# Output projection of a decoder layer: seven half-size products per pair of row blocks instead of eight

## The chip, the core and the metric

The kernel runs on one core of a Trainium2 chip. A core has five engines, each with a queue of its own that is worked off in order: TensorE (PE in the profile; PEld is its loading of weights), VectorE (DVE), ScalarE (ACT), GpSimd (POOL) and SyncE (SP), which here issues all DMA transfers. An engine that meets an instruction whose operands are not ready waits, and so does everything that is queued behind it. Engines wait for each other by semaphores. Matmuls write to PSUM, eight banks of 128 x 512 float32; everything else lies in SBUF.

The metric is the device time of one execution in microseconds (us).

## What is computed

One decoder layer on a sequence of 4096 rows of width 1024. Cut to what matters here:

```python
q_a, k_a, v_a, g_a, q_b, k_b, v_b, g_b, r_b = split_cols(x @ w_in, IN_SPLITS)
out_a = sliding_window_attention(rope(q_a), rope(k_a), v_a, sinks) * silu(g_a)   # 512 columns
out_b = norm(gla_chunked(q_b, k_b, v_b, log_a)) * silu(g_b)                      # 512 columns
mix = concatenate([out_a, out_b]) @ w_out                                        # (4096 x 1024) @ (1024 x 1024)
x = layer_norm(ALPHA * x + mix, ln_g, ln_b)
```

All of it is float32. A matmul takes its operands as float32r, a shorter form, so the kernel splits each operand into a rounded part h and the rest l and adds three products, hh + hl + lh.

## The kernel before

The 4096 rows are 32 blocks of 128 (NB = 32). Three stages follow each other: sliding-window attention over all blocks, gated linear attention (GLA) over all blocks, and then the output projection with residual and layer norm, which is what the change rewrites.

The first two stages leave their halves of the projection's input, transposed, in DRAM: `mixd[n][0]` and `mixd[n][1]`, each 128 x 4 x 128, for block n. The projection then takes one block after another (lines 729 to 764). It loads both halves into `mr` and the block's residual rows into `xr`; `split` makes `mh` (a cast on ACT, line 98) and `ml` (a subtraction on DVE, line 103). For each half of the 1024 output columns `project` (line 128) runs 8 chunks of 3 matmuls of 128 x 512 into one PSUM bank, `py`: 48 matmuls a block. DVE adds ALPHA times the residual from the bank (line 745) and takes statistics (746, 747); `rsqrt_eps` (767) is a few one-column instructions on DVE and ACT. Then ACT scales the block (761), POOL multiplies by `lg` (762), DVE adds `lb` (763), and SP stores it (764). The last block does its tail on DVE in two halves (755, 756).

The weights of the projection are loaded by `load_group` (line 106) near the end of the GLA stage, one half of the columns after `b_split_v` of the last block and one after its `b_gate`: 16 raw tiles, each with a cast on ACT and a subtraction on DVE or POOL.

Tiles come from pools with a fixed number of buffers for each tag. A tile whose buffer is still in use waits for its last reader: `xraw`, `xh` and `xl` have two buffers each, `xr` and `y` two, each PSUM tag (`pj`, `tp`, `c`, `d`) two. Code is written in program order, and a scheduler then sets the order of each engine's queue; the queue is fixed when the program is built.

Of the kernel before, what the change touches and what calls it, by code (L numbers as in the profile page):

```python
# [9 lines left out]
F32 = mybir.dt.float32  # L10
F32R = mybir.dt.float32r
# [8 lines left out]
P = 128  # L20
D = 1024
# [16 lines left out]
# column groups of the input projection, in the order the host lays them out  # L38
# [3 lines left out]
# constant columns: identity, cumulative-sum matrix, halves, causal mask, attention masks  # L42
# [8 lines left out]
def layer_kernel(  # L51
# [23 lines left out]
    xp = ctx.enter_context(tc.tile_pool(name="xp", bufs=2))  # L75
    ps = ctx.enter_context(tc.tile_pool(name="ps", bufs=2, space=PSUM))
# [18 lines left out]
    def split(hdst, ldst, src, heng, leng):  # L95
        """src = hdst + ldst exactly: a rounded part and the rest."""
# [8 lines left out]
    # ---- weights: slot s of chunk k holds (h, l) of one column group  # L105
    def load_group(wr, src, c0, n, slot, width, early=False):
        hs, ls = [], []
        for k in range(NK):
            raw = wr.tile([P, 512], F32, tag="wraw", name=f"wraw{slot}_{k}")
# [18 lines left out]
    def project(dst, x, wg, n, k0=0, k1=NK):  # L128
        """Chunks k0..k1 of one column group's product with a block of rows."""
        hs, ls = wg  # L130
        for k in range(k0, k1):
            a, b = x[0][:, k, :], x[1][:, k, :]
            pe.matmul(dst[:, :n], a, hs[k][:, :n], start=(k == 0), stop=False)  # L133
            pe.matmul(dst[:, :n], a, ls[k][:, :n], start=False, stop=False)  # L134
            pe.matmul(dst[:, :n], b, hs[k][:, :n], start=False, stop=(k == NK - 1))  # L135

    # ================= sliding-window attention =================
    with ExitStack() as pa:
        wr = pa.enter_context(tc.tile_pool(name="wra", bufs=6))
# [9 lines left out]
        wkv = load_group(wr, w_a, 512, 256, 1, 272, True)  # L149

        # rotary tables: [position in block, block, (cos | cos)], (sin | sin)
# [31 lines left out]
        # ---- constants  # L183
# [14 lines left out]
        # ---- up-projection of the decay, bias as one more row; rows: (h, b_h), h, (l, b_l), l  # L198
# [31 lines left out]
        def a_kv(n, pkv, qk):  # L230
            """Rotary; the values' parts."""
# [19 lines left out]
        def a_turn_k(n, kk):  # L251
            """Keys with dims on the partitions, twice."""
# [8 lines left out]
        def a_turn_q(n, qk):  # L261
            """Queries with dims on the partitions, (h ; l) stacked."""
# [21 lines left out]
        def a_scores(n, qs):  # L284
            """Four steps, one for each bank of two heads; the last gives the probabilities."""
# [109 lines left out]
        for n in range(NB):  # L395
# [19 lines left out]
            if n == NB - 2:  # L415
                wb["q"] = load_group(wr, w_b, 0, 272, 1, 272)
# [430 lines left out]
```

## Time and profile before

| | us |
|---|---|
| median of three runs | 1766.86 |
| lowest and highest | 1766.32, 1768.08 |
| span of the profiled execution | 1766.5 |
| PE busy in it | 1733.4 (98%) |
| DVE busy | 1057.4 (60%) |
| ACT busy | 802.2 (45%) |
| POOL busy | 457.0 (26%) |

The profiled execution ran within 0.4 us of the median, so sums are made against its span. Shares of the whole span are averages over three stages: attention to about 670 us, GLA to about 1405 us, the projection from there on. The granted clock of PE is full in nearly all slices. Since matmuls are pipelined, the duration of a matmul's row is longer than the time that one costs; the distance between starts shows that.

### The profile page before, as it was taken

How to read it: one execution, taken by the hardware profiler on the slowest of the kernel's cores; microseconds unless marked ns; L12 is line 12 of the kernel's file. 1: busy time of each engine (PE TensorE's matmuls, PEld its weight loads, DVE VectorE, ACT ScalarE, POOL GpSimd, SP SyncE). 2: the span in 40 equal slices, each digit the busy share in tenths (PEclk: the TensorE clock that was granted, in tenths of full speed). 3: DMA queues.
4: the chain of work that ended last, by engine and by line, in shares of the span. 5: the costliest groups of instructions: out<-in, count | busy, mean ns of one | idle time of the engine just before them, and what ended most of it. 6: DMA issues, size and time to landing. Idle time of an engine off the chain costs nothing.

```text
span 1766.5 us, 27174 instructions
## 1 busy us (share of the span) xinstructions
PE 1733.4 (98%) x9978; PEld 1503.2 (85%) x9978; DVE 1057.4 (60%) x2738; ACT 802.2 (45%) x2032; POOL 457.0 (26%) x633
## 2 busy tenths in 40 slices
PE   7999999999999999999999999999999899999998
PEld 5788888888888887899999999999999788888886
DVE  6766666666666677555555555555555655555555
ACT  5555554555555466444444444444444622222221
POOL 3222222222222243322222222222222412222221
PEclk9999999999999999999999999999999999999999
DMA  6211111111111132111111111111111354444442
GB/s 202 90 37 37 37 37 42 48 37 37 37 37 37 43 103 69 34 37 37 37 37 37 37 37 37 37 37 37 37 37 37 114 171 145 146 147 148 144 143 83
DMA packets 48649, 120.00 MB, mean 68 GB/s; under 512 B 5698, under 2 KB 9092, under 8 KB 48516
## 3 DMA queue, kind: packets, MB, share of 16 engines
q1 hardware_dynamic: 48516, 118.27, 20.2%
q8 instruction: 78, 1.28, 0.3%
q14 instruction: 55, 0.45, 0.1%
HBM read 84.70 MB, written 33.55 MB: 67 GB/s over the span
## 4 chain that ended last, share of the span: by engine, by line
PE 57%; DVE 1%; DMA 0%; ACT 0%; issue 0%; POOL 0%; DVEq 0%; ACTq 0%
PE py L133 7%; PE py L135 7%; PE py L134 7%; PE bv L133 3%; PE bg L133 3%; PE bg L135 3%; PE bg L134 3%; PE bv L134 3%; PE bv L135 3%; PE bq L133 2%; PE bq L134 2%; PE bq L135 2%; PE bk L135 2%; PE bk L134 2%; PE bk L133 2%; PE to L669 1%
## 5 line engine op out<-in xcount | busy, mean ns | idle before, releaser
L134 PE MATMUL py<-wl,mh 128*128 128x512 f32 x512 | 199.9, 390 | 0.0
L135 PE MATMUL py<-wh,ml 128*128 128x512 f32 x512 | 199.8, 390 | 0.0
L133 PE MATMUL py<-wh,mh 128*128 128x512 f32 x512 | 199.8, 390 | 0.0
L339 POOL TENSOR_SCALAR s<-s,rec 128x256 f32<-128x256 f32 x256 | 124.4, 502 | 280.4 <-DVE ngm L327 217.4
L331 ACT ACTIVATE s<-s,ngm 128x256 f32<-128x256 f32 x256 | 127.2, 498 | 137.6 <-DVE ngm L327 132.7
L762 POOL TENSOR_TENSOR y<-y,lg 128x1024 f32<-128x1024 f32 x31 | 74.3, 2396 | 268.1 <-ACT y L761 253.4
L100 POOL TENSOR_SCALAR xh<-xraw 128x512 fp32r<-128x512 f32 x126 | 78.6, 641 | 203.6 <-PE pg L134 191.7
L520 POOL TENSOR_TENSOR qp<-bqs,ee 128x256 f32<-128x256 f32 x32 | 24.3, 759 | 377.2 <-ACT ee L515 365.1
L314 DVE CUSTOM_DVE_ANT_0 s<-psc,msk 128x256 f32<-128x256 f32 x256 | 97.9, 420 | 31.2 <-PE psc L304 30.3
L103 DVE TENSOR_TENSOR pl<-pt,ph 128x512 fp32r<-128x512 f32 x128 | 85.6, 688 | 49.6 <-ACT ph L98 47.4
L135 PEld LDWEIGHTS py<-wh,ml 128*128 128x128 f32 x512 | 96.5, 188 | 20.1
L134 PEld LDWEIGHTS py<-wl,mh 128*128 128x128 f32 x512 | 96.4, 188 | 20.0
L133 PEld LDWEIGHTS py<-wh,mh 128*128 128x128 f32 x512 | 96.5, 189 | 19.8
L133 PE MATMUL pg<-wh,xh 128*128 128x512 f32 x256 | 112.5, 440 | 0.8 <-DVE vv L247 0.8
L133 PE MATMUL pq<-wh,xh 128*128 128x512 f32 x256 | 104.5, 408 | 6.3 <-ACT wh L98 6.1
L98 ACT CAST ph<-pt 128x512 fp32r<-128x512 f32 x128 | 72.1, 588 | 84.5 <-PE pt L353 82.8
L135 PE MATMUL pq<-wh,xl 128*128 128x512 f32 x256 | 103.3, 403 | 3.3 <-DVE xl L103 3.3
L133 PE MATMUL bg<-wh,xh 128*128 128x512 f32 x256 | 106.1, 414 | 0.0
L133 PE MATMUL bv<-wh,xh 128*128 128x512 f32 x256 | 105.4, 412 | 0.0
L98 ACT CAST mh<-mr 128x1024 fp32r<-128x1024 f32 x32 | 33.7, 1054 | 155.3 <-PE py L134 155.3
L134 PE MATMUL pq<-wl,xh 128*128 128x512 f32 x256 | 103.0, 402 | 0.1
L135 PE MATMUL pg<-wh,xl 128*128 128x512 f32 x256 | 101.1, 395 | 0.0
(224 smaller groups left out, 5126.5 us busy)
## 6 DMA issues: line engine op xcount, KB each, us to landing
xraw<-in_xt_dram SPq DMA_DIRECT2D x64, 512.0 KB, 3.5
mr<-mx SPq DMA_DIRECT2D x64, 256.0 KB, 3.5
xr<-in_xn_dram SPq DMA_DIRECT2D x32, 512.0 KB, 3.5
out_dram<-y SPq DMA_DIRECT2D x31, 512.0 KB, 2.6
mx<-att SPq DMA_DIRECT2D x32, 256.0 KB, 2.0
mx<-mb SPq DMA_DIRECT2D x32, 256.0 KB, 2.1
wraw<-in_w_a_dram SPq DMA_DIRECT2D x16, 256.0 KB, 4.4
wraw<-in_w_b_dram SPq DMA_DIRECT2D x16, 256.0 KB, 3.9
```

Of the source, the lines that this page charges most:

```text
L98: act.copy(hdst, src)
L100: pool.tensor_scalar(hdst, src, 1.0, 1.0, ALU.mult, ALU.mult)
L103: leng.tensor_tensor(ldst, src, hdst, ALU.subtract)
L133: pe.matmul(dst[:, :n], a, hs[k][:, :n], start=(k == 0), stop=False)
L134: pe.matmul(dst[:, :n], a, ls[k][:, :n], start=False, stop=False)
L135: pe.matmul(dst[:, :n], b, hs[k][:, :n], start=False, stop=(k == NK - 1))
L314: dve.tensor_tensor_reduce(out=s, in0=psc[:, e * 256 : (e + 1) * 256], in1=mask, scale=0.125, scalar=NEG, op0=ALU.add, op1=ALU.max, accum_ ...
L331: act.activation(sc[i], sc[i], AF.Exp, bias=ngm[:, h : h + 1], accum_out=den[:, h : h + 1])
L339: pool.tensor_scalar(sc[i], sc[i], rec[:, h : h + 1], 1.0, ALU.mult, ALU.mult)
L520: pool.tensor_tensor(qp, B[n]["q"], ee, ALU.mult)
L669: pe.transpose(to[:, hs], og[:, hs], ident)
L762: pool.tensor_tensor(y, y, lg, ALU.mult)
```

## The change

Two row blocks are now taken together. The pair's input is a 2 x 2 arrangement A of pieces with 128 rows and 512 columns (a11, a12 of the even block, a21, a22 of the odd one), the weights a 2 x 2 arrangement B of 512 x 512. One level of Strassen's scheme, in Winograd's form, gives the four output pieces from seven products instead of eight. It needs four sums of pieces of A in each pair (s1 to s4), four of pieces of B (once, when the weights are loaded), and seven on the output side, of which three are made by letting a second product accumulate in the bank of a first one.

- **Weights.** `w_split` makes seven operands (h, l) for each of four chunks: 28 casts on ACT, 28 subtractions on DVE and 16 sums on POOL, instead of 16 casts and 16 subtractions. Chunks 0 and 1 come in the last GLA block, chunk 2 after it, chunk 3 when the projection's pools are open.
- **A pair's input.** `pair_load` loads both blocks and makes the sums on POOL; `pair_parts` makes seven (h, l) pieces of 128 x 512 in two buffers of `xh` and `xl`; `pair_late` makes the last three of them later.
- **Products.** `product` is 4 chunks of 3 matmuls: 84 matmuls for a pair.
- **Output.** `residual` loads the two blocks' rows into `y` itself and scales them by ALPHA on ACT. u1 is a copy of the first bank (ACT), u2 and u3 are running sums (DVE); three sums onto `y` are made on POOL, four on DVE. The layer norm is as before.
- **Elsewhere.** The GLA weights for q and k become one group of 528 columns, loaded at the seam of the first two stages (k's was loaded in block 2 before). Some buffers change their number: `wra` 6 to 5, `wrb` 3 to 4, `ah`, `al`, `gw` 2 to 1, `y` 2 to 4.

```diff
-    wkv = load_group(wr, w_a, 512, 256, 1, 272, True)
+    wkv = load_group(wr, w_a, 512, 256, 1, 528, True)
...
-                wb["q"] = load_group(wr, w_b, 0, 272, 1, 272)
-            if n == 2:
-                wb["k"] = load_group(wr, w_b, 272, 256, 3, 256)
+                wb["qk"] = load_group(wr, w_b, 0, 528, 1, 528)
...
+        def w_split(k, q, extra=None):
+            r11, r12, r21, r22 = q
...
+            part(0, r11, dve)
+            pool.tensor_tensor(r11, r12, r11, ALU.subtract)
+            pool.tensor_tensor(r12, r22, r12, ALU.subtract)
+            part(6, r22, dve)
+            pool.tensor_tensor(r22, r22, r11, ALU.subtract)
+            part(3, r11, dve)
+            part(4, r21, dve)
+            pool.tensor_tensor(r21, r21, r22, ALU.subtract)
+            part(2, r12, dve)
+            part(1, r22, dve)
+            part(5, r21, dve)
...
+        def pair_parts(p, i, srcs):
+            h = xp.tile([P, NK, P], F32R, tag="xh", name=f"mh{p}_{i}")
+            l = xp.tile([P, NK, P], F32R, tag="xl", name=f"ml{p}_{i}")
+            for c, src in zip((lo, hi), srcs):
+                split(h[:, c], l[:, c], src, act, dve)
+            return [(h[:, c], l[:, c]) for c, _ in zip((lo, hi), srcs)]
+
+        def pair_load(p):
+            ra = xp.tile([P, NK, P], F32, tag="xraw", name=f"ma{p}")
+            rb = xp.tile([P, NK, P], F32, tag="xraw", name=f"mb{p}")
+            for r, n in ((ra, 2 * p), (rb, 2 * p + 1)):
+                sp.dma_start(r[:, :4, :], mixd[n][0])
+                sp.dma_start(r[:, 4:, :], mixd[n][1])
...
+            pool.tensor_tensor(s1, rb[:, lo], rb[:, hi], ALU.add)
+            pool.tensor_tensor(s2, s1, ra[:, lo], ALU.subtract)
+            pool.tensor_tensor(rb[:, lo], ra[:, lo], rb[:, lo], ALU.subtract)
+            parts = pair_parts(p, 0, (ra[:, lo], s2))
+            pool.tensor_tensor(s2, ra[:, hi], s2, ALU.subtract)
+            parts += pair_parts(p, 1, (rb[:, lo], s1))
+            return parts, (ra[:, hi], rb[:, hi], s2)
+
+        def pair_late(p, made):
+            parts, (a12, a22, s4) = made
+            return parts + pair_parts(p, 2, (a12, a22)) + pair_parts(p, 3, (s4,))
...
             if last:
-                wo[0] = load_group(wr, w_o, 0, 512, 0, 512)
+                w_split(0, w_load(wr, 0))
             pk = bank("pj", f"bk{n}")
-            project(pk, x, wb["k"], 256)
+            project(pk, x, wb["qk"], 256, off=272)
+            if last:
+                w_split(1, w_load(wr, 1))
...
+        first = pair_load(0)
+        w_split(2, w_load(wr, 2))
         b_out(NB - 1)
         b_store(NB - 1)
...
+        w_split(3, w_load(wr, 3), c1)
...
+                y = c4.tile([P, D], F32, tag="y", name=f"y{n}")
+                sp.dma_start(y, xn[n * P : (n + 1) * P, :])
+                act.mul(y, y, ALPHA)
...
+                b7, b5 = bank("c", f"b7_{p}"), bank("d", f"b5_{p}")
+                b2, b3, b4 = b1, b5, b7
+                product(b1, made[0][0], 0)
+                product(b6, made[0][1], 1)
+                ops = pair_late(p, made)
+                product(b7, ops[2], 2)
+                product(b5, ops[3], 3)
+
+            act.copy(u1, b1)
+            dve.tensor_tensor(u2, u1, b6, ALU.add)
+            dve.tensor_tensor(u3, u2, b7, ALU.add)
+
+            pool.tensor_tensor(y1[:, HI], y1[:, HI], u3, ALU.add)
+            dve.tensor_tensor(y1[:, HI], y1[:, HI], b5, ALU.add)
+            stats(n1, y1, st1, 1)
+            pool.tensor_tensor(y1[:, LO], y1[:, LO], u2, ALU.add)
+            pool.tensor_tensor(y0[:, HI], y0[:, HI], u2, ALU.add)
+            if p + 1 < NB // 2:
+                nxt = pair_load(p + 1)
...
+                product(b2, ops[4], 4, more=True)
+                product(b4, ops[5], 5, more=True)
+                product(b3, ops[6], 6, more=True)
+            dve.tensor_tensor(y0[:, LO], y0[:, LO], b2, ALU.add)
+            stats(n0, y0, st0, 0)
+            dve.tensor_tensor(y1[:, LO], y1[:, LO], b4, ALU.add)
+            stats(n1, y1, st1, 0)
+            normed(n1, y1, st1)
+            dve.tensor_tensor(y0[:, HI], y0[:, HI], b3, ALU.add)
+            stats(n0, y0, st0, 1)
+            normed(n0, y0, st0, p == NB // 2 - 1)
```

What stands in the queues, once with blocks 23 to 25 before and pairs 11 to 13 after (blocks 22 to 26); lines are those of each kernel's own file. First SP's queue in the middle of the projection, before: `mr` are a block's two input halves, `xr` its residual rows.

```order
L731 DMA mr24_18379<-mx24_0_117 128x512
L732 DMA mr24_18379<-mx24_1_118 128x512
L764 DMA out_0_dram<-y20_18064 128x1024
L734 DMA xr23_18301<-in_xn_dram 128x1024
L731 DMA mr25_18460<-mx25_0_119 128x512
L732 DMA mr25_18460<-mx25_1_120 128x512
L764 DMA out_0_dram<-y21_18145 128x1024
```

SP's queue in the middle of the projection after the change: `ma` and `mb` are the inputs of a pair's even and odd block, `y26` and `y27` receive residual rows.

```order
L853 DMA out_0_dram<-y23_18462 128x1024
L733 DMA ma13_18719<-mx26_0_124 128x512
L853 DMA out_0_dram<-y22_18459 128x1024
L734 DMA ma13_18719<-mx26_1_125 128x512
L733 DMA mb13_18720<-mx27_0_126 128x512
L734 DMA mb13_18720<-mx27_1_127 128x512
L827 DMA y26_18817<-in_xn_dram 128x1024
L827 DMA y27_18820<-in_xn_dram 128x1024
```

Before, a store of block 20 or 21 stands among loads for blocks 23 to 25. Now three of pair 13's four input loads stand right behind the store of block 22, which is written while pair 12 is worked on.

POOL's queue at the change from the GLA stage to the projection, before (from `y0` on there is one such row for each block, and nothing else):

```order
L103 TENSOR_TENSOR wl2_3_16327<-wraw2_3_16324,wh2_3_16326 128x512
L103 TENSOR_TENSOR wl2_5_16339<-wraw2_5_16336,wh2_5_16338 128x512
L626 TENSOR_TENSOR gw31_16298<-gw31_16298,gs31_16297 128x512
L103 TENSOR_TENSOR wl2_7_16351<-wraw2_7_16348,wh2_7_16350 128x512
L762 TENSOR_TENSOR y0_16444<-y0_16444,lg_16431 128x1024
L762 TENSOR_TENSOR y1_16525<-y1_16525,lg_16431 128x1024
```

POOL's queue in one pair of the projection after the change (the same nine rows come again for each pair from the third on):

```order
L737 TENSOR_TENSOR s1_12_18546<-mb12_18541 128x512
L738 TENSOR_TENSOR s2_12_18547<-s1_12_18546,ma12_18540 128x512
L739 TENSOR_TENSOR mb12_18541<-ma12_18540,mb12_18541 128x512
L741 TENSOR_TENSOR s2_12_18547<-ma12_18540,s2_12_18547 128x512
L851 TENSOR_TENSOR y23_18462<-y23_18462,lg_16480 128x1024
L891 TENSOR_TENSOR y25_18641<-y25_18641,u2_12_18647 128x512
L892 TENSOR_TENSOR y24_18638<-y24_18638,u2_12_18647 128x512
L851 TENSOR_TENSOR y22_18459<-y22_18459,lg_16480 128x1024
L888 TENSOR_TENSOR y25_18641<-y25_18641,u3_12_18648 128x512
```

Two multiplications by `lg` in a pair have become nine instructions, and those of pair 11's blocks (22 and 23) now stand behind the input sums of pair 12 and around its first output sums.

DVE's queue around the addition of `lb` (line 763) in the middle of the projection, before:

```order
L760 SCALAR_TENSOR_TENSOR nb22_18292<-mv22_18228,crs22_18284 128x1
L745 SCALAR_TENSOR_TENSOR y23_18307<-xr23_18301,py23_0_18310 128x512
L763 TENSOR_TENSOR y22_18226<-y22_18226,lb_16432 128x1024
L746 BN_STATS cst23_18308<-y23_18307 128x6
L745 SCALAR_TENSOR_TENSOR y23_18307<-xr23_18301,py23_1_18337 128x512
L746 BN_STATS cst23_18308<-y23_18307 128x6
L103 TENSOR_TENSOR ml25_18466<-mr25_18460,mh25_18465 128x1024
```

DVE's queue around the two additions of `lb` (now line 852) for blocks 23 and 22, after the change; `cnt`, `crs` and `nb` are one-column steps of the norm, the `ml12` the l parts of pair 12's last pieces:

```order
L921 TENSOR_TENSOR cnt22_18625<-crs22_18624 128x1
L922 SCALAR_TENSOR_TENSOR cnt22_18625<-cnt22_18625,mv22_18622 128x1
L923 SCALAR_TENSOR_TENSOR crs22_18624<-cnt22_18625,crs22_18624 128x1
L849 SCALAR_TENSOR_TENSOR nb22_18632<-mv22_18622,crs22_18624 128x1
L885 TENSOR_TENSOR u2_12_18647<-u1_12_18646,b6_12_18650 128x512
L852 TENSOR_TENSOR y23_18462<-y23_18462,lb_16481 128x1024
L104 TENSOR_TENSOR ml12_2_18678<-ma12_18540,mh12_2_18677 128x512
L104 TENSOR_TENSOR ml12_2_18678<-mb12_18541,mh12_2_18677 128x512
L852 TENSOR_TENSOR y22_18459<-y22_18459,lb_16481 128x1024
L886 TENSOR_TENSOR u3_12_18648<-u2_12_18647,b7_12_18651 128x512
L889 TENSOR_TENSOR y25_18641<-y25_18641,b5_12_18652 128x512
```

The end of the previous pair's layer norm (blocks 22 and 23) now stands between u2 and u3 of pair 12, and ahead of the l parts that the pair's last three products read.

## Rows read from the trace of the kernel before

**Rows 1.** The page, part 1: busy us (share, instructions) by engine.

```profile
PE 1733.4 (98%) x9978; PEld 1503.2 (85%) x9978; DVE 1057.4 (60%) x2738; ACT 802.2 (45%) x2032; POOL 457.0 (26%) x633
```

**Rows 2.** The chain of waits from 1390 us to the end, shares by line.

```profile
by line: PE py L133 30.7%; PE py L135 30.7%; PE py L134 30.6%; DMA wraw<-in_w_o_dram 1.0%; issue 0.6%; DVE wl L103 0.6%; DVE og L659 0.4%; DVE nt L772 0.4%; DVE y L755 0.4%; ACT wh L98 0.3%; DVE y L756 0.2%; DVE cst L746 0.2%; DVE btl L103 
```

**Rows 3.** Twenty blocks: us; PE, PEld, DVE, ACT, POOL busy (x); clock, DMA, GB/s.

```profile
1443.80:1661.40 217.60, 217.60 (x962) 180.18 (x961) 118.69 (x241) 54.06 (x81) 47.93 (x20) 1.00 0.43 145
```

**Rows 4.** Waits of that stage: engine, line, releaser; us, times, longest.

```profile
POOL y L762 <- ACT y L761: 229.1, 27, 8.5
...
DVE y L745 <- PE py L135: 69.1, 55, 1.4
```

**Rows 5.** Timeline of PE, projection: start us, duration us, instruction.

```profile
1561.13 0.39 PE L133 MATMUL py<-wh,mh 128*128 128x512 f32 x1
...
1561.81 0.39 PE L133 MATMUL py<-wh,mh 128*128 128x512 f32 x1
```

**Rows 6.** Groups by form, those twenty blocks: busy us, mean ns, idle before.

```profile
L762 POOL TENSOR_TENSOR y<-y,lg 128x1024 f32<-128x1024 f32 x20 | 47.9, 2396 | 169.7 <-ACT y L761 169.7
L746 DVE BATCH_NORM_STATS2 cst<-y 128x6 f32<-128x512 f32 x41 | 28.3, 691 | 0.7
...
L761 ACT ACTIVATE y<-y,nb,crs 128x1024 f32<-128x1024 f32 x20 | 24.9, 1243 | 16.2 <-DVE nb L760 16.2
L763 DVE TENSOR_TENSOR y<-y,lb 128x1024 f32<-128x1024 f32 x20 | 24.5, 1226 | 35.0 <-POOL y L762 35.0
...
L772 DVE TENSOR_TENSOR cnt<-crs 128x1 f32<-128x1 f32 x20 | 3.2, 160 | 10.1 <-ACT crs L771 10.1
```

**Rows 7.** Groups by form, loading of projection weights, 1370 to 1412 us.

```profile
L103 POOL TENSOR_TENSOR wl<-wraw,wh 128x512 fp32r<-128x512 f32 x8 | 10.7, 1335 | 11.2 <-ACT wh L98 11.2
L98 ACT CAST wh<-wraw 128x512 fp32r<-128x512 f32 x16 | 9.8, 617 | 7.1 <-DMA wraw<-in_w_o_dram 6.7 <-PE bv L135 0.4
L103 DVE TENSOR_TENSOR wl<-wraw,wh 128x512 fp32r<-128x512 f32 x8 | 7.6, 951 | 3.6 <-ACT wh L98 3.5
```

**Rows 8.** The tile `wl` there: ns min/median/max, first and last start.

```profile
L103 DVE TENSOR_TENSOR wl<-wraw,wh x8: 670/693/1705, 1381.5 to 1408.5; 128x512 fp32r<-128x512 f32 x8
L103 POOL TENSOR_TENSOR wl<-wraw,wh x8: 1282/1292/1634, 1383.0 to 1410.8; 128x512 fp32r<-128x512 f32 x8
```

**Rows 9.** Timeline of DVE in that stretch.

```profile
1393.68 2.37 DVE L103 TENSOR_TENSOR wl<-wraw,wh 128x512 fp32r<-128x512 f32 x2
...
1408.46 0.67 DVE L103 TENSOR_TENSOR wl<-wraw,wh 128x512 fp32r<-128x512 f32 x1
1409.06 0.67 DVE L103 TENSOR_TENSOR al<-am,ah 128x512 fp32r<-128x512 f32 x1
```

**Rows 10.** Timeline of POOL in that stretch.

```profile
1393.87 1.63 POOL L103 TENSOR_TENSOR wl<-wraw,wh 128x512 fp32r<-128x512 f32 x1 [3.02 <-ACT wh L98]
...
1408.67 2.21 POOL L626 TENSOR_TENSOR gw<-gw,gs 128x512 f32<-128x512 f32 x1 [0.87 <-ACT gs L619]
```

**Rows 11.** The tile `st` in the GLA stage: ns min/median/max.

```profile
L535 DVE TENSOR_SCALAR st<-tot,dd x62: 272/514/760, 729.3 to 1397.6; 128x128 f32<-128x128 f32 x62
```

**Rows 12.** DMA issues of the projection: KB each, median us to landing.

```profile
out_dram<-y SPq DMA_DIRECT2D x28, 512.0 KB, 2.6
...
mr<-mx SPq DMA_DIRECT2D x52, 256.0 KB, 3.6
```

**Rows 13.** Timeline of SP's queue, one issue in the projection.

```profile
1565.63 0.42 SPq L732 DMA_DIRECT2D mr<-mx  x1
```

**Rows 14.** Columns as in Rows 3, just behind a wait of PE.

```profile
1405.00:1408.40 3.40, 3.40 (x12) 2.90 (x11) 3.40 (x6) 3.40 (x7) 1.29 (x1) 0.50 0.60 216
```

**Rows 15.** Waits of PE, 1380 to 1420 us.

```profile
PE pat L576 <- ACT qbh L561: 3.6, 1, 3.6
```

**Rows 16.** Timeline of the kernel's end.

```profile
1758.10 0.39 PE L135 MATMUL py<-wh,ml 128*128 128x512 f32 x1
...
1762.85 0.99 SPq L757 DMA_DIRECT2D out_dram<-y  x2
```

More of the change, by code (lines that the diff above doesn't have):

```diff
@@ L126, in load_x, with project @@
         return h, l
[L128 removed]
+    def project(dst, x, wg, n, k0=0, k1=NK, off=0):
         hs, ls = wg
+        c = slice(off, off + n)
         for k in range(k0, k1):
             a, b = x[0][:, k, :], x[1][:, k, :]
[L133 to L135 removed]
+            pe.matmul(dst[:, :n], a, hs[k][:, c], start=(k == 0), stop=False)
+            pe.matmul(dst[:, :n], a, ls[k][:, c], start=False, stop=False)
+            pe.matmul(dst[:, :n], b, hs[k][:, c], start=False, stop=(k == NK - 1))
     with ExitStack() as pa:
[L139 removed]
+        wr = pa.enter_context(tc.tile_pool(name="wra", bufs=5))
         e1 = pa.enter_context(tc.tile_pool(name="e1", bufs=1))
@@ L728, in layer_kernel, with product, residual, stats @@
         sp.dma_start(lb, ln_b.partition_broadcast(P))
-        for n in range(NB):
-            raw = xp.tile([P, NK, P], F32, tag="xraw", name=f"mr{n}")
-            sp.dma_start(raw[:, :4, :], mixd[n][0])
-            sp.dma_start(raw[:, 4:, :], mixd[n][1])
-            xr = c2.tile([P, D], F32, tag="xr", name=f"xr{n}")
-            sp.dma_start(xr, xn[n * P : (n + 1) * P, :])
-            mh = xp.tile([P, NK, P], F32R, tag="xh", name=f"mh{n}")
-            ml = xp.tile([P, NK, P], F32R, tag="xl", name=f"ml{n}")
-            split(mh, ml, raw, act, dve)
-            y = c2.tile([P, D], F32, tag="y", name=f"y{n}")
-            st = c2.tile([P, 2, 6], F32, tag="st", name=f"cst{n}")
-            mv = c2.tile([P, 2], F32, tag="mv", name=f"mv{n}")
-            for i in range(2):
-                s = slice(512 * i, 512 * i + 512)
-                py = bank(("pj", "tp")[n % 2], f"py{n}_{i}")
-                project(py, (mh, ml), wo[i], 512)
-                dve.scalar_tensor_tensor(y[:, s], xr[:, s], ALPHA, py, ALU.mult, ALU.add)
-                dve.bn_stats(st[:, i, :], y[:, s])
+        def product(dst, x, op, k0=0, k1=4, more=False):
+            xh_, xl_ = x
+            for k in range(k0, k1):
+                h, l = wo[k][op]
+                a, b = xh_[:, k, :], xl_[:, k, :]
+                pe.matmul(dst, a, h, start=(not more and k == 0), stop=False, skip_group_check=more)
+                pe.matmul(dst, a, l, start=False, stop=False, skip_group_check=more)
+                pe.matmul(dst, b, h, start=False, stop=(k == 3), skip_group_check=more)
+        LO, HI = slice(0, 512), slice(512, 1024)
+        def residual(p):
+            ys = []
+            for i in range(2):
+                n = 2 * p + i
+                y = c4.tile([P, D], F32, tag="y", name=f"y{n}")
+                sp.dma_start(y, xn[n * P : (n + 1) * P, :])
+                act.mul(y, y, ALPHA)
+                ys.append(y)
+            return ys
+        def stats(n, y, st, i):
+            dve.bn_stats(st[:, i, :], y[:, 512 * i : 512 * i + 512])
+        def normed(n, y, st, tail=False):
+            mv = c2.tile([P, 2], F32, tag="mv", name=f"mv{n}")
             dve.bn_aggr(mv, st.rearrange("p a b -> p (a b)"))
@@ L751, in layer_kernel @@
             rows = slice(n * P, (n + 1) * P)
-            if n == NB - 1:
-                for i in range(2):
-                    s = slice(512 * i, 512 * i + 512)
+            if tail:
+                for s in (LO, HI):
                     dve.scalar_tensor_tensor(y[:, s], y[:, s], mv[:, 0:1], lg[:, s], ALU.subtract, ALU.mult)
```

75 lines of the change are left out of this document (64 added, 11 removed).

## The prediction

> **What bounds the kernel now.** First the page's busy shares: PE works 98% of the span [rows 1]. Then the chain of waits from 1390 us on: three matmul lines of `project` carry 92% of it, so in the projection nothing but PE sets the time [rows 2]. Then twenty blocks in its middle: 217.60 us, or 10.88 us a block, PE busy in all of them, at full clock (2.4 GHz), while DVE is busy for 118.7 us, ACT for 54.1 and POOL for 47.9 [rows 3]. The waits there are of engines that wait for PE, or for each other behind it [rows 4]. Starts of matmuls three apart lie 0.68 us apart, so one costs 0.2267 us, whatever its row says [rows 5]; 96 in two blocks make 21.76, which is the 2 x 10.88 above. The other engines have half their time free, but the change takes from PE and gives to them, so I need what two blocks ask of each, and in which order.
>
> **What it removes.** 12 of 96 matmuls per pair of blocks: 84 x 0.2267 = 19.04 us instead of 21.76. If PE stayed the bound that is 16 x 2.72 = 43.5 us.
>
> **What it adds, as busy time.** Per pair POOL gets seven sums of 128x512 (four input, three output) beside its two multiplications by `lg`. Such an instruction takes 1.29 us undisturbed [rows 8], `lg` 2.40 [rows 6]: 7 x 1.29 + 2 x 2.40 = 13.8 us. That is under 19, and DVE's and ACT's sums are too. By shares alone the change would pay.
>
> **What the shares don't show: DVE and POOL hold each other up.** Subtractions of one kind in one stretch take between 0.67 and 1.7 us on DVE, and 1.28 to 1.63 on POOL [rows 8]. The timelines tell which: two on DVE took 2.37 us together when a POOL instruction started 0.2 us after the first one [rows 9, 10]; and where two ran on DVE back to back at 0.67 each, from 1408.46 on, POOL's `gw`, started 0.2 us behind the first, took 2.21 us, that is 1.29 and the rest of both [rows 9, 10]. A small `tensor_scalar` of GLA shows the same: 0.27 us at best, 0.51 median, 0.76 at most [rows 11]. So I count a DVE instruction with two SBUF inputs and a two-input POOL instruction as excluding each other, the later one waiting for the whole of the earlier and for what DVE runs directly behind. DVE instructions that read PSUM or one input stay at 0.69 in all of the projection [rows 6], and I leave them free.
>
> The Trainium skill ("SBUF — State Buffer", section "Who interferes with whom") says that a DVE instruction with two SBUF inputs contends with a GpSimd instruction that reads SBUF, and that the loser "fully blocks" rather than slowing down. The single rows agree; the group's mean, 951 ns beside a median of 693 [rows 7, 8], reads like a partial price of 0.26 us. By the rule a pair takes about 29 us, by the mean about 24.3.
>
> Of that exclusive time a pair needs, beside POOL's 13.8, seven subtractions of 0.69, two additions of `lb` at 1.23 and eight one-column steps at 0.16 [rows 6, 8]: 8.6 on DVE, together 22.4 us. That alone is over PE's 19.04, and over the 21.76 of before, where the same sum is 4.8 + 6.2 = 11.0.
>
> **The chain through a pair.** It isn't only a sum: the queues tie it into a loop. From the order of the queues in a pair, with durations of rows:
> (a) DVE adds `lb` to the even block of the pair before, 1.23 [rows 6].
> (b) SP waits for that to store the block; behind the store stand three of the next pair's four input loads. Issues are 0.4 apart [rows 13], and a load lands 3.6 after its issue, a store of 512 KB taking 2.6 beside it [rows 12]: 3 x 0.4 + 3.6 = 4.8 at least; all four transfers share the same engines, so I take 5.6 (bounds 4.6 and 6).
> (c) POOL makes s1 and s2, both of which need the last load: 2 x 1.29, and half a microsecond behind DVE: 3.1.
> (d) ACT casts s2: 0.62 [rows 7].
> (e) DVE: half a microsecond behind POOL's third sum, then three subtractions, three statistics at 0.69, an addition from the bank at 0.69 and seven small steps, up to `nb` of the odd block; less what back-to-back instructions overlap (0.6 instead of 0.69 from start to start [rows 9]): 5.7.
> (f) ACT scales the odd block: 1.24 [rows 6].
> (g) POOL multiplies it by `lg`: 2.40. Meanwhile DVE's small steps for the even block stand still.
> (h) DVE: those small steps, u2, `lb` of the odd block, two subtractions, one behind the other: 0.8 + 0.69 + 1.23 + 1.3, less overlap 3.7. POOL's sums with u2 stand still behind them.
> (i) POOL: two sums with u2, then `lg` of the even block: 2 x 1.29 + 2.40 = 5.0. Then (a) again.
> Sum: 1.23 + 5.6 + 3.1 + 0.62 + 5.7 + 1.24 + 2.40 + 3.7 + 5.0 = 28.6, and nine handovers of about 0.05: **29 us a pair**. Bounds: 27.3 with the loads at 4.6 and no half microsecond in (c) or (e) where the other engine happens to be done, 29.9 with loads at 6 and one more sum delayed. The first pairs are lighter, since no norm stands before them; on average I take 28.7. Against 21.76 that is 6.9 us more in each of some 14 intervals: **+97 us** (bounds +78 and +114). PE's busy time falls by 43.5 us as planned, and this buys nothing: PE waits some 9.7 us in each pair.
>
> **From GLA into the projection.** Before, 16 subtractions were shared by DVE and POOL there. Now 28 on DVE (0.69) and 16 sums on POOL (1.29) exclude each other: 19.3 + 20.6 = 40 us where before it was 16. They stand in the last blocks of GLA, whose own chain has DVE and POOL steps, and before the first products, which need all chunks; chunk 3's loads stand behind the store of block 31's GLA part. I take **+22** (bounds +8, if most of the 24 us runs beside GLA's matmuls, and +30).
>
> **The end.** Before, 8.4 us passed from the start of the last matmul to the end of the span [rows 16]. The last product is now followed by the odd block's norm ahead of the even one's on DVE, about 5 us of statistics, small steps and half-size sums; and before that the last pair's products wait as in any pair. **+11** (bounds +3, +14).
>
> **Elsewhere.** k's GLA weights are loaded with q's at the seam rather than in block 2; nothing waited long at either place: **-3** (bounds -6, +3). Casts on ACT and the ALPHA multiplications (0.62 and 1.24 at most) lie beside DVE's work in (e); if that is shorter they come onto the path, one microsecond a pair at most.
>
> Sum: 1766.5 + 97 + 22 + 11 - 3 = 1893.5, and with the 0.4 us that the median lies above the profiled span about **1895**.
>
> **Rivals.**
> 1. *PE stays the bound* (the other side: faster). The place is PE's wait for the pieces of the sums; the point from which it decides is a loop of 19.04 us, ten less than mine. For it speaks that every engine's own share fits. It needs the loads to be issued ahead of the stores and both exclusions to vanish: without (b) and the lock waits 29 becomes 29 - 5.6 - 1.0 - 3.7 = 18.7. The queues put the loads behind. Time: 1766.5 - 43.5 + 8 + 3 = 1734. Chance 0.06.
> 2. *DVE and POOL share, only slowed down.* Then the half microseconds of (c) and (e) fall, and (h) runs beside (g) and (i): 29 - 1.0 - 3.7 = 24.3. For it speaks the mean of 951; against it the single rows. 14 x (24.3 - 21.76) = 36, 12 for the seam, 6 for the end: 1766.5 + 36 + 12 + 6 - 3 = 1817. Chance 0.16.
> 3. *The clock falls.* PE now waits in each pair, some 4 us before the fifth product and 3 before the sixth by the loop above. After its one wait of 3.6 us before, the granted clock was 0.50 (1.2 GHz) until 1408.40, for 3.4 us [rows 14, 15], which costs 1.7 us of matmuls. A pair has 9.7 us to spare on PE, so most of it is hidden; but the products that feed the last sums are on the path. One or two falls a pair with 1.7 us each would add 24 to 48 us: 1918 to 1942. Chance 0.08.
> That the change doesn't do what it says is excluded for the matmuls: the queue of PE holds 84 in each pair.
>
> **How the numbers follow.** The forecast has 0.70. It and rival 3 are slower, rival 2 is too; faster is rival 1 with 0.06; no change, within 0.2% (about what a measurement of this kernel can tell), needs a loop of some 21 us between rivals 1 and 2: 0.02. The range goes from 1817, the middle of rival 2, to 1930, the middle of rival 3; it leaves out rival 1, half of rival 2, half of rival 3 and the little between, 0.2 in all. The forecast's own bounds (78 to 114, 8 to 30, 3 to 14, -6 to 3) lie inside it where not all are at one end.
>
> **What would show it.** In the profile after: first products of successive pairs 28 to 29 us apart; PE busy in two thirds of the projection, waiting before the first product and before the fifth and sixth for casts or subtractions; DVE and POOL busy rows that look longer than 0.69, 1.23 and 1.29, with maxima near the sum of two; the chain of waits going through SP's loads, `s2`, `lb` and `lg` in place of `py`. A period near 24 with long rows would be rival 2; PE above 95% rival 1; a granted clock of 0.5 in much of the projection rival 3. The loop is wrong if loads land in under 4.6 us behind `lb`, or if the chain shows casts or the ALPHA multiplications instead.

## The result, and the profile after the change

The changed kernel takes 1883.41 us (median; 1880.87 to 1883.81) against 1766.59 beside it, a ratio of 1.0657 [1.0644, 1.0669]: 117 us slower, 12 us under the forecast of 1895 and inside its range. Its profiled execution has a span of 1882.0 us, 115.5 more than that of before.

The page, busy time, share and instructions of each engine:

```profile
PE 1749.7 (93%) x9786; PEld 1491.3 (79%) x9786; DVE 1199.8 (64%) x2869; ACT 871.3 (46%) x2164; POOL 640.4 (34%) x749
```

TensorE has 192 matmuls fewer than in [rows 1], and yet 16 us more busy time, for the larger part because of the slow clock below. VectorE works 142 us longer, GpSimd 183.

Ten pairs in the middle of the projection: the stretch, its length, busy time (instructions) of PE, PEld, DVE, ACT and POOL, granted clock, DMA share, GB/s:

```profile
1480.00:1760.00 280.00, 225.97 (x841) 173.30 (x840) 194.78 (x310) 93.32 (x161) 157.77 (x92) 0.88 0.32 113
```

In [rows 3] PE was busy throughout at clock 1.00. Now it is busy for 226 of 280 us, at a mean clock of 0.88. POOL has risen from 22% to 56% of the stretch, DVE from 55% to 70%: no engine is full.

The pace of the pairs, by POOL's sum with u3 (line 888), which each pair has once; the first and the last of sixteen:

```profile
1448.45 1.30 POOL L888 TENSOR_TENSOR y<-y,u 128x512 f32<-128x512 f32 x1 [1.23 <-DVE u L886]
...
1863.12 1.28 POOL L888 TENSOR_TENSOR y<-y,u 128x512 f32<-128x512 f32 x1 [1.94 <-DVE u L886]
```

(1863.12 - 1448.45) / 15 = 27.64 us a pair, where it was 21.76. That is 15 x 5.88 = 88 of the 115.5 us. The other 27 lie ahead of the first of these two points and behind the second.

The chain of waits through one pair (start, duration, what; small pieces left out):

```profile
1526.03 1.24 DVE y L852
1527.28 0.34 SPq L853
...
1528.96 4.01 DMA mb<-mx
...
1533.14 1.26 POOL s L737
...
1534.48 1.63 POOL s L738
1536.13 0.63 ACT mh L99
1536.78 1.12 DVE ml L104
...
1540.04 1.19 DVE ml L104 x2
...
1541.94 1.13 issue
...
1543.29 2.39 DVE cnt L921
...
1546.16 0.69 DVE u L885
...
1546.92 2.18 POOL y L891
...
1550.79 2.78 POOL y L851
1553.60 1.24 DVE y L852
```

From one addition of `lb` to the next, 27.57 us, and not one matmul among them. It reads: `lb` of the even block, its store on SP, the loads behind that store, the input sums on POOL, a cast, DVE's steps to the scale of the odd block, ACT's scaling of it (the 1.13 us of "issue"), one small step that lasts as long as POOL's `lg`, u2, POOL's two u2 sums and the second `lg`. In the pairs between 1606 and 1720 us the same view names matmuls on part of the way (43% of that stretch); the first experiment tests that.

How VectorE and GpSimd meet, in the timelines of the same pair, first POOL, then DVE:

```profile
1543.24 2.41 POOL L851 TENSOR_TENSOR y<-y,lg 128x1024 f32<-128x1024 f32 x1 [3.95 <-ACT crs L920]
1546.92 2.18 POOL L891 TENSOR_TENSOR y<-y,u 128x512 f32<-128x512 f32 x1 [1.28 <-DVE u L885]
1549.07 1.73 POOL L892 TENSOR_TENSOR y<-y,u 128x512 f32<-128x512 f32 x1
```

```profile
1541.15 0.15 DVE L921 TENSOR_TENSOR cnt<-crs 128x1 f32<-128x1 f32 x1
...
1543.29 2.38 DVE L921 TENSOR_TENSOR cnt<-crs 128x1 f32<-128x1 f32 x1 [1.40 <-ACT crs L920]
...
1546.76 1.22 DVE L852 TENSOR_TENSOR y<-y,lb 128x1024 f32<-128x1024 f32 x1
1547.89 1.76 DVE L104 TENSOR_TENSOR ml<-ma,mh 128x512 fp32r<-128x512 f32 x1
```

The step `cnt` on one column takes 0.15 us at 1541.15, and 2.38 us at 1543.29, when it starts 0.05 us behind `lg`'s 2.41. Then DVE's `lb` starts first, and POOL's sum, 0.16 us behind it, takes 2.18 us instead of 1.29; behind that DVE's subtraction takes 1.76 instead of 0.69, and POOL's next sum 1.73. The two engines take turns, and each pays for the other's instruction. The Trainium skill ("SBUF — State Buffer", section "Who interferes with whom") calls this contention "an exclusive lock" and counts a DVE instruction with two SBUF inputs against a GpSimd instruction that reads SBUF; this trace agrees, with 2.38 against 0.15 us as its plainest row.

What PE waits for in that pair, and its granted clock behind the second wait (timeline of PE; a stretch with PE's busy time, clock, DMA share and GB/s):

```profile
1549.71 0.50 PE L817 MATMUL b<-woh,ml 128*128 128x512 f32 x1 [2.73 <-DVE ml L104]
...
1555.57 0.76 PE L815 MATMUL b<-woh,mh 128*128 128x512 f32 x1 [3.26 <-DVE u L886]
```

```profile
1555.57:1558.50 2.93, 2.93 (x7) 0.50 0.96 327
```

2.73 us before the l parts of the fifth product, 3.26 before the sixth, which waits for u3. Behind the second wait the clock stands at 0.50 (1.2 GHz) for some 3.3 us, and seven matmuls start 0.43 us apart instead of 0.23. In other pairs this comes behind the first wait, and in some it lasts through both: of the 84 matmuls of a pair some ten start 0.43 us apart (140 in the fourteen pairs from 1480 us on). So rows of matmuls get longer and PE's busy time rises although it does less.

The way into the projection, waits of PE from 1380 to 1480 us:

```profile
PE pat L576 <- ACT qbh L561: 5.2, 1, 5.2
PE b L815 <- ACT woh L99: 4.9, 3, 3.6
```

PE waits for casts of weights there, which [rows 15] did not have. The end, timeline:

```profile
1869.92 0.40 PE L817 MATMUL b<-woh,ml 128*128 128x512 f32 x1
...
1877.94 0.96 SPq L846 DMA_DIRECT2D out_dram<-y  x2
```

The last matmul starts 12.1 us before the end of the span; in [rows 16] it was 8.4.

### The profile page after: what moved, and what is told of

The parts are those of the page before. It is cut to its first block, busy times and chain, and to the rows that moved or that the text cites. A ratio compares the mean times of both kernels' runs of the same rounds, so it can differ in the third digit from the quotient of the medians.

```text
span 1882.0 us, 27240 instructions
## 1 busy us (share of the span) xinstructions
PE 1749.7 (93%) x9786; PEld 1491.3 (79%) x9786; DVE 1199.8 (64%) x2869; ACT 871.3 (46%) x2164; POOL 640.4 (34%) x749
## 4 chain that ended last, share of the span: by engine, by line
PE 72%; DVE 10%; POOL 8%; DMA 4%; issue 2%; ACT 2%; SPq 1%; POOLq 0%; DVEq 0%; ACTq 0%
PE psc L306 3%; PE bv L135 3%; PE pt L355 3%; PE bv L136 3%; PE bg L135 3%; PE bg L137 3%; PE bv L137 3%; PE bg L136 3%; PE pg L135 3%; PE pg L137 3%; PE pg L136 3%; PE pq L135 3%; PE pq L137 3%; PE pq L136 3%; DMA mb<-mx 3%
## 5 line engine op out<-in xcount | busy, mean ns | idle before, releaser
L817 PE MATMUL b<-woh,ml 128*128 128x512 f32 x448 | 195.4, 436 | 48.4 <-DVE ml L104 48.3
L815 PE MATMUL b<-woh,mh 128*128 128x512 f32 x448 | 195.6, 437 | 37.9 <-DVE u L886 30.5
L816 PE MATMUL b<-wol,mh 128*128 128x512 f32 x448 | 192.4, 429 | 3.7 <-DVE wol L104 3.7
L817 PEld LDWEIGHTS b<-woh,ml 128*128 128x128 f32 x448 | 94.1, 210 | 80.3 <-DVE ml L104 58.4
L815 PEld LDWEIGHTS b<-woh,mh 128*128 128x128 f32 x448 | 94.2, 210 | 69.8 <-issue 37.8
L816 PEld LDWEIGHTS b<-wol,mh 128*128 128x128 f32 x448 | 94.0, 210 | 27.7 <-DVE wol L104 6.2
L851 POOL TENSOR_TENSOR y<-y,lg 128x1024 f32<-128x1024 f32 x31 | 81.1, 2617 | 68.1 <-ACT y L850 64.1
L136 PE MATMUL bv<-wl,xh 128*128 128x512 f32 x256 | 101.1, 395 | 0.0
```

Source lines behind the costliest of these rows:

```text
L136: pe.matmul(dst[:, :n], a, ls[k][:, c], start=False, stop=False)
L815: pe.matmul(dst, a, h, start=(not more and k == 0), stop=False, skip_group_check=more)
L816: pe.matmul(dst, a, l, start=False, stop=False, skip_group_check=more)
L817: pe.matmul(dst, b, h, start=False, stop=(k == 3), skip_group_check=more)
L851: pool.tensor_tensor(y, y, lg, ALU.mult)
```

## The experiments

All are complete kernels but the first and the fourth. The order of the queues decides here, and the scheduler that makes it answers to any edit with another order everywhere. So in all but one the order of SP, ACT, DVE and POOL in the projection is written out: a small class `Recorder` notes each instruction that an engine is given, and at the end every queue is chained in the order of a table. Those instructions carry the line of `Recorder` (L64) in the profile; their tiles' names tell them apart.

```diff
+    act, dve, pool, sp = (Recorder(e, tapes[k]) for k, e in ...)
...
+        for k, seq in ORDER.items():
+            row = [tapes[k][marks[k] + i] for i in seq]
+            for a, b in zip(row, row[1:]):
+                after(b, a)
```

### Is it PE after all?

```diff
                 pe.matmul(dst, a, h, start=(not more and k == 0), stop=False, skip_group_check=more)
-                pe.matmul(dst, a, l, start=False, stop=False, skip_group_check=more)
+                if pair_now[0] == 0:
+                    pe.matmul(dst, a, l, start=False, stop=False, skip_group_check=more)
                 pe.matmul(dst, b, h, start=False, stop=(k == 3), skip_group_check=more)
```

> The changed kernel with every queue held in its own order, and without the middle one of the three matmuls (h of the input by l of the weights) in pairs 1 to 15: 56 instead of 84 matmuls a pair, so that part of each product is not computed; nothing else is left out. My theory (the loop through SP's loads, POOL's sums and the exclusion of DVE and POOL sets 27.64 us a pair, PE only waits): the distance of pairs stays at 27.4 to 27.7 us and the time falls by no more than the shorter last two products, 1 to 5 us, to 1878 to 1883. Rival (PE sets it after all, with the half clock behind its waits, as the chain of waits names it in some pairs): 28 x 0.2267 = 6.35 us less a pair, 15 x 6.35 = 95 us, about 1790.

1879.88 us (1.0643 [1.0625, 1.0661]). POOL's first and last sum with u3:

```profile
1448.35 1.30 POOL L64 TENSOR_TENSOR y<-y,u 128x512 f32<-128x512 f32 x1 [1.23 <-DVE u L64]
...
1859.32 1.28 POOL L64 TENSOR_TENSOR y<-y,u 128x512 f32<-128x512 f32 x1 [1.94 <-DVE u L64]
```

27.40 us a pair. A third of PE's work is gone from fifteen pairs, 95 us at full clock, and 3.5 us come of it. PE does not set the pace, nor does its slow clock; where the chain of waits named matmuls, another wait must have ended close behind them.

### Loads ahead of the stores

The order of SP's queue alone; for each pair:

```diff
-    store 1 (p-1), load a lo (p+1), store 0 (p-1), load a hi, load b lo, load b hi (p+1)
+    load a lo, load a hi, load b lo, load b hi (p+1), store 1, store 0 (p-1)
```

> Complete kernel, all queues as in the changed kernel but SP's: the two stores of a pair stand behind the four loads of the pair after next instead of before three of them. My theory: loads are then issued when the late l parts are made (1551.4 in the pair that ends at 1556.5) and not after `lb` and the store (1555.2), and s1 starts when POOL is free, 1556.8 instead of 1560.7; the pair gets 3 to 3.9 us shorter, 23.7 to 24.7, the time 1883 - 14 x 3.3 = about 1837 (1825 to 1845). Rival (PE or the exclusion alone sets the pace, loads are hidden behind it): 1883, no change.

1856.03 us (1.0503 [1.0488, 1.0519]), 27 us less; 46 were expected.

```profile
1451.05 1.29 POOL L64 TENSOR_TENSOR y<-y,u 128x512 f32<-128x512 f32 x1 [1.22 <-DVE u L64]
...
1834.83 1.28 POOL L64 TENSOR_TENSOR y<-y,u 128x512 f32<-128x512 f32 x1 [1.94 <-DVE u L64]
```

25.59 us a pair: 2.05 less, where 3 to 3.9 were expected. The loads are on the path, and the rival of no change is out. What is late next stands in the timeline of a pair behind the wait for u3:

```profile
1558.58 0.69 DVE L64 TENSOR_TENSOR y<-y,b 128x512 f32<-128x512 f32 x1 [0.59 <-PE b L847]
...
1564.27 0.59 ACT L64 COPY u<-b 128x512 f32<-128x512 f32 x1 [0.97 <-PE b L847]
```

POOL no longer waits for loads. But DVE waits 0.59 us for the sixth product, and ACT 0.97 for the next pair's first one, which stand behind the half-clock stretch. With the loads out of the way the products are next on the chain (PE's matmuls 22% of it from 1480 to 1840 us). In other pairs it goes through a store and the residual rows that are loaded into the buffer which that store frees (12%):

```profile
1577.82 4.57 DMA out_dram<-y
1582.46 4.27 DMA y<-in_xn_dram
```

That these two give back the rest of the gain is read from the chain and was not tried by itself. The rival with PE was wrong for the changed kernel and has a part in this one.

### One-column steps on ACT

```diff
-    dve.tensor_tensor(nt, rs, rs, ALU.mult)
-    dve.scalar_tensor_tensor(nt, nt, -0.5, ms, ALU.mult, ALU.mult)
-    dve.scalar_tensor_tensor(rs, nt, 1.5, rs, ALU.add, ALU.mult)
+    act.activation(nt, rs, AF.Square)
+    act.activation(nt, nt, AF.Identity, scale=ms)
+    act.activation(nt, nt, AF.Copy, bias=1.5, scale=-0.5)
+    act.activation(rs, rs, AF.Identity, scale=nt)
```

(shortened, and `nb` likewise)

> Complete kernel, all queues in the order of the changed kernel, but the four one-column steps of the norm (`cnt` twice, `crs`, `nb`) are made on ACT from one-input instructions instead of on DVE. My theory: `cnt` waits 2.2 us behind `lg` because DVE and POOL exclude each other; ACT's steps don't wait, u2 is ready some 3 us earlier, and POOL goes from `lg` to the u2 sums at once: 1.2 us less a pair, at most 1.9; 26.0 to 26.8 us, time about 1865 (1855 to 1870). Rival (those 2.4 us are no exclusion but the price of a one-column step on a slow stretch, or lie beside the path): 1883 or, as ACT's steps take 0.2 each and are more, up to 10 us slower.

1877.70 us (1.0626 [1.0610, 1.0642]): 6 us less, a third of what was expected. POOL's timeline from `lg` of the odd to `lg` of the even block:

```profile
1572.13 2.40 POOL L64 TENSOR_TENSOR y<-y,lg 128x1024 f32<-128x1024 f32 x1 [4.83 <-ACT y L64]
1574.49 3.47 POOL L64 TENSOR_TENSOR y<-y,u 128x512 f32<-128x512 f32 x2
1577.92 2.81 POOL L64 TENSOR_TENSOR y<-y,lg 128x1024 f32<-128x1024 f32 x1
```

From the start of the first `lg` to the end of the second it now takes 8.6 us (1580.73 - 1572.13); in the changed kernel 10.3 (1553.57 - 1543.24). So the wait behind `lg` was real, and 1.7 us of it went, as foretold. But six steps of 0.2 to 0.3 us on ACT now stand before its scaling of the odd block, from the `Exp` of `crs` to `lg` 4.3 us instead of 3.4, and that gave back half. And DVE's second subtraction now waits out the second `lg`, so that `lb` starts 0.47 us behind it instead of 0.03. A pair takes 27.15 us, 0.5 less. The mechanism held; my account of its gain forgot the road to it.

### The sums of weight pieces left out

```diff
             part(0, r11, dve)
-            pool.tensor_tensor(r11, r12, r11, ALU.subtract)
-            pool.tensor_tensor(r12, r22, r12, ALU.subtract)
             part(6, r22, dve)
-            pool.tensor_tensor(r22, r22, r11, ALU.subtract)
...
-            pool.tensor_tensor(r21, r21, r22, ALU.subtract)
```

> The projection's queues as in the changed kernel, but the 16 sums of weight pieces on POOL are left out, so the products take unsummed pieces as weights; all loads, casts and subtractions remain. My theory: of the 22 us that I put on the way from GLA into the projection the larger part is these sums (16 x 1.29 = 20.6 us of POOL, exclusive with DVE's 28 subtractions): 8 to 16 us less, 1867 to 1875, with pairs unchanged at 27.6. Rival (the loads of the last chunk behind the last store set it): under 3 us less, 1880 or more.

1869.76 us (1.0583 [1.0565, 1.0602]), 14 us less; the pace stays at 27.60. The first sum with u3:

```profile
1431.24 1.29 POOL L64 TENSOR_TENSOR y<-y,u 128x512 f32<-128x512 f32 x1 [1.23 <-DVE u L64]
```

It starts 17 us earlier (1431.24 for 1448.45); this profile is of the fastest of four runs, which lie between 1866.97 and 1872.94. So the sums of weight pieces make up 14 (by the medians) to 17 (by the profiles) of the 27 us that lie outside the fifteen pairs; 10 or a little more remain for the casts and subtractions and for the end.

### The order of the queues alone

The same instructions on the same engines; the table has loads ahead of stores, u2 and u3 as soon as their banks are ready, and the steps of the previous pair's norm in between.

> Complete kernel with exactly the instructions of the changed one on the same engines; only the order of the four queues in the projection is another, written by hand: loads ahead of stores, u2 and u3 as soon as their banks are ready, the steps of the norm of the pair before between them. My theory after three runs: the loop through the queues is one of order, and what is left under it is the exclusive time of DVE and POOL, 22.4 us a pair by the rows of before (21.6 if instructions overlap by a tenth of a microsecond at each change of hands). So 21.6 to 22.5 instead of 27.64 a pair, 15 x 5.6 = 84 us less: 1800 (1785 to 1815), still slower than before. Rival A (half clock of PE and waits inside the products set about 25, as in the run with loads first): 1840 to 1850. Rival B (exclusion costs less than thought, the order was all): PE's 19.04 a pair, 1755.

1785.66 us (1.0103 [1.0088, 1.0118]). `lg` of one block, thirteen pairs apart, and the stretch between:

```profile
1485.82 2.44 POOL L64 TENSOR_TENSOR y<-y,lg 128x1024 f32<-128x1024 f32 x1 [3.01 <-ACT y L64]
...
1759.51 2.45 POOL L64 TENSOR_TENSOR y<-y,lg 128x1024 f32<-128x1024 f32 x1 [3.03 <-ACT y L64]
```

```profile
1450.00:1750.00 300.00, 284.46 (x1204) 222.12 (x1204) 287.03 (x443) 127.21 (x223) 236.17 (x128) 1.00 0.43 144
```

(1759.51 - 1485.82) / 13 = 21.05 us a pair, less than the 21.76 of before, and 98 us less in all. That is most of the loss of 117 us, and nothing of it was in the work that was added: the order had made a loop of work that could have been side by side. My theory's number for what is left, the exclusive time of DVE and POOL, was 21.6 to 22.5; it is 21.05, and DVE is busy or held up in 287 of 300 us. But the chain of waits from 1500 to 1750 us names PE, and PE's timeline shows one wait in each pair:

```profile
by line: PE b L845 32.6%; PE b L847 31.1%; PE b L846 30.7%; ACT u L64 2.8%; ACT mh L64 2.5%; issue 0.3%
```

```profile
1543.46 0.50 PE L845 MATMUL b<-woh,mh 128*128 128x512 f32 x1 [1.20 <-ACT mh L64]
```

PE works for 19.9 us without a wait, and then waits 1.2 us for a cast that stands in ACT's queue behind the copy of the first bank (u1). By the chain, PE and that cast set this pace, nearer to rival B than to my theory; the exclusive time fits into 21.05 us, and that my number came out so near was luck. What keeps this version above 1766 is no longer the pairs, which gain 15 x 0.71 us, but the 28 us at their two ends.

### The sums moved into the GLA stage, and the order again

```diff
+        def input_sums(p):
+            t = [wr.tile([P, 528], F32, tag="wraw", name=f"ps{p}_{i}")[:, :512] for i in range(4)]
...
+                step(s1, a21, a22, ALU.add, 0),
+                step(s2, s1, a11, ALU.subtract, 1),
+                step(a21, a11, a21, ALU.subtract, 2),
+                step(a12, a12, s2, ALU.subtract, 3),
```

Each `step` is a sum on POOL and a store to DRAM; the sums of weight pieces go the same way, and the projection loads seven pieces a pair and 28 of the weights.

> Complete kernel; the four sums of each pair's input and the 16 sums of weight pieces are made on POOL during the GLA stage, where PE is busy throughout, and stored in DRAM; the projection loads them (seven pieces a pair, in four buffers). Order of the queues by the scheduler. POOL's exclusive time in a pair falls by 4 x 1.29 = 5.2 us to 17.2, and the way into the projection loses 16 x 1.29 us of POOL. My theory (order of queues sets the loop, not the sum): a pair still takes 23.5 to 25 us, since u3 still stands behind `lb` of the pair before; 1883 - 15 x 3.4 - 12 = 1820 (1800 to 1835). Rival (the exclusive sum sets the pace): 17.2 is below PE's 19.04, so PE sets it, 1745.

1840.93 us (1.0426 [1.0407, 1.0445]); a pair takes 23.5 us (twelve pairs, by `lg`: 282.1 us). The rival, that the exclusive sum sets the pace, is out: 17.2 us of it a pair, and still 23.5. PE's waits:

```profile
PE b L870 <- DVE u L946: 36.4, 14, 4.3
PE tr L492 <- DVE r L485: 11.2, 13, 0.9
```

The first row is the old queue order: the sixth product waits for u3, up to 4.3 us. The second is new, in GLA, which ends 11 us later than in the changed kernel (the last transpose of block 31 starts at 1437.2 us instead of 1426.1). That is about half of the 21 us by which the time is above the expected 1820; where the rest comes from was not traced.

> Complete kernel; the sums moved into the GLA stage as in the kernel before this one, and the queues of the projection in an order written by hand. Exclusive time 17.2 us and DVE's 16 are both under PE's 19.04. My theory: 19.1 to 19.8 us a pair, PE busy nearly throughout at full clock; GLA as long as before; 1735 to 1760, faster than the kernel before by 0.5 to 1.7%. Rival (contention costs more than row by row, or the sums delay GLA, 1 us in each of its 32 blocks): 1765 to 1790.

1786.02 us (1.0110 [1.0093, 1.0127]). A pair takes 19.43 us (ten pairs, by `lg`), as foretold, and the total is 26 us above the expected range. For 17 us of it GLA got longer: the last transpose of block 31 starts at 1435.0 us instead of 1418.0 in the kernel before.

> As the kernel before this one, but the three output sums of each pair stand on DVE instead of POOL (0.69 instead of 1.29 us, and next to instructions that don't exclude each other). Exclusive time 17.2 - 3 x 1.29 + 3 x 0.65 = 15.3, DVE busy 17.8 of 19.04. My theory: 19.0 to 19.4 us a pair, up to 8 us less than with POOL: 1730 to 1752. Rival (DVE, now the fuller engine, is late for PE in each pair): 20 or more a pair, 1760.

1777.57 us (1.0060 [1.0045, 1.0075]); 19.33 us a pair (twelve pairs). DVE is not late for PE. The total is again 26 us above the range, 18 of them for the same reason (the last transpose at 1435.8). Two stretches of GLA, where PE was busy throughout before, are 4.4 and 5.5 us short, and then the transposes `to` of the last blocks (ns min/median/max, first and last start):

```profile
900.00:1100.00 200.00, 195.65 (x1242) 174.56 (x1241) 116.32 (x256) 90.45 (x229) 81.47 (x86) 1.00 0.31 104
1100.00:1380.00 280.00, 274.54 (x1744) 245.32 (x1744) 166.02 (x357) 125.95 (x318) 107.20 (x113) 1.00 0.28 90
...
L739 PE MATMUL to<-cs,og x8: 270/272/327, 1411.6 to 1435.8; 128*128 128x128 f32 x8
```

POOL's timeline in one GLA block (names: `s` and `ps` are sums, `gw` a step of the block's gate):

```profile
1029.52 1.32 POOL L64 TENSOR_TENSOR s<-ps,ps 128x512 f32<-128x512 f32 x1
...
1035.44 1.29 POOL L64 TENSOR_TENSOR gw<-gw,gs 128x512 f32<-128x512 f32 x1
```

Four sums in a row stood in front of `gw`, beside DVE's subtractions for the next block, and DVE's `r`, for which PE waits, came 0.9 us late in 13 blocks. Behind `gw` POOL had nothing to do for 12 us.

```diff
+                some(3 if len(todo) > 4 else 2, B[n - 1]["tots"] if n > 1 else None)
```

`some` now issues two or three sums in each block, the first of them behind DVE's `tot`.

> Complete kernel, as the one before it (sums moved into the GLA stage, hand order, output sums on DVE), but the sums of input and weight pieces stand behind `tot` and `gw` in each GLA block, where POOL is idle for 12 us, instead of in front of `gw`. In the kernel before this one PE waited 11.1 us in 13 waits for DVE's `r`, which stands behind DVE instructions that the sums hold up, and was 3 to 6 us short of full in each of three stretches of GLA. My theory (exclusion again, only in another stage): GLA takes no longer than in the kernel before, 11 to 15 us less: 1762 to 1768, that is no slower than the kernel before. Rival (the sums cost GLA the same wherever they stand, by their loads and stores in SP's queue): 1775 to 1780.

1762.80 us (0.9978 [0.9969, 0.9987]). The same place in another block, and two stretches of this run:

```profile
1003.38 1.29 POOL L64 TENSOR_TENSOR gw<-gw,gs 128x512 f32<-128x512 f32 x1 [2.82 <-ACT r L64]
1006.11 1.28 POOL L64 TENSOR_TENSOR s<-s,ps 128x512 f32<-128x512 f32 x1 [1.43 <-DVE tot L64]
```

```profile
900.00:1100.00 200.00, 200.00 (x1281) 180.16 (x1280) 108.46 (x263) 92.93 (x234) 85.14 (x91) 1.00 0.34 110
...
1500.00:1740.00 240.00, 238.48 (x1032) 193.32 (x1031) 211.13 (x419) 117.99 (x197) 60.90 (x25) 1.00 0.57 196
```

GLA has lost nothing in its stretch, its last transpose starts at 1420.7 us, 15 earlier than in the kernel before this one, the projection runs at 19.46 us a pair with PE busy in 238.5 of 240 us, and the kernel is a little faster than before the change. The same sums cost 15 us in front of `gw` and next to nothing behind it.

> As the kernel before it, with another hand order: in the first two pairs ACT's ALPHA multiplications stand behind the casts that PE waits for, and the loads of `lg`, `lb` and of pair 1's residual rows behind the loads of pair 1's input. In the kernel with the output sums on DVE, ACT waited at 1446 to 1454 for residual rows while PE waited 3.8 us for a cast behind it. My theory: 3 to 8 us less than its neighbour, 1755 to 1764, faster than the kernel before by 0.2 to 0.6%. Rival (the weight loads set the start: 28 pieces of 256 KB instead of 16): the same time as its neighbour within 2 us.

1761.59 us (0.9973 [0.9962, 0.9983]): the same as its neighbour within the noise. The rival's time holds; the order of the first pairs' steps was not what cost. Of the 43.5 us that 192 matmuls are worth, 15 x 2.30 = 34.5 (by the neighbour's 19.46) are now collected in the fifteen pairs, and 28 go to the two ends. The sums of weight pieces are gone from POOL there, but 28 loads stand in place of 16. That these loads set it is likely from PE's waits for weight casts (7.7 us in this run), and was not tried by itself.

## Where the prediction was right, and where not

- **The bound, and that PE's saving buys nothing.** Right. PE waits in each pair, and a third less of its work changes the pair by 0.24 us.
- **The loop.** Right as a whole and in its order: 27.64 us measured, 28.7 forecast; 88 us in fifteen intervals for 97 in fourteen. By its steps in the pair shown, forecast and measured: (a) 1.23, 1.24; (b) 5.6, 5.8; (c) 3.1, 3.0; (d) 0.62, 0.65; (e) 5.7, 5.1; (f) 1.24, 1.3; (g) 2.40, 2.4; (h) 3.7, 1.3; (i) 5.0, 6.7.
- **The step that failed is (h).** I let the later instruction wait for the earlier one "and for what DVE runs directly behind", from one row of `gw` [rows 10]. Here the engines take turns: POOL's first u2 sum got in behind `lb`, before the two subtractions. What (h) lost, 2.4 us, came back in part in (i), where the sums are lengthened: the sum of both is 8.0 for 8.7. That the total came so near owes something to this.
- **Exclusion.** Right in kind: the rows of `cnt` and of the u2 sums show it, and moving the steps or the sums moved the time. As a floor the sum of rows, 22.4 us a pair, was too high: the kernel with another order takes 21.05, and there the chain names PE and a cast, not the exclusion.
- **The way in and the ends.** 22 + 11 - 3 = 30 us forecast, 27 measured outside the fifteen pairs, with 14 to 17 of them for the weight sums. The end alone was mis-sized: 3.7 us more from the last matmul on, not 11; part of what I put there is already counted as the last pair's wait. Elsewhere: block 30's transposes stand at 1393.25 us in place of 1394.41, a gain of 1.2 for a forecast of 3.
- **Rival 3.** The clock falls as it said, behind one of the two long waits or through both, and costs some ten matmuls a pair 0.2 us each. It was all but hidden (a third of the matmuls less changed the pair by 0.24 us); it shows as soon as the loads are out of the way.
- **Rival 2** has no support: single rows are held up for whole instructions.
- **Rival 1** lost as the kernel stands, but its condition, loads ahead of stores and the exclusions side by side with PE, is what the later experiments built. I gave the queues as fixed, which they were; a reader should see that the forecast was one of an order, not of the scheme.
- **Signs.** I looked for PE waits before the first product; there are hardly any (2.0 us in all, 0.8 at most), since the slow sixth and seventh products run into it. PE was to be busy in two thirds of the projection; it shows 81%, mostly because half-clock rows are longer. My chances add up to 1.02.

## What to carry to other kernels

Work taken off a full engine and given to others that have time left is not free when the others share something: add up what they exclude each other for (here the sum of single rows, 22.4 us, was above the 21.05 us that a pair takes in another order), and follow one period of the loop through the queues, store before load included. When a change loses, hold its instructions fixed and change only their order before giving the scheme up; here that was worth 98 of 117 us. And look for where the helper engines stand idle for long in a stage whose bound is elsewhere: the same sums cost 15 us in one place of a block and next to nothing in the other.

## What was not expected of the hardware

- Two engines that exclude each other take turns even when one has its next instruction ready: `lb`, a sum, a subtraction, a sum, a subtraction, 1.2 to 2.2 us each by their rows, in every pair from the third on. In GLA of the kernel before, one POOL instruction had waited for two of DVE's [rows 9, 10]. What decides between the two stayed open.
- A one-column step can last 2.4 us when it falls behind a long instruction of the other engine, sixteen times its own 0.15.
- Matmul rows can add up to more busy time with 192 instructions fewer: 1749.7 us for 1733.4, mostly by half-clock stretches behind waits of up to 3.3 us.
